# Lp pooling on one core: Square, reduce and Sqrt twice as wide, and the last store moved to the SP queue

## Chip, cores and metric

One core of one Trainium2 chip (trn2). Of its engines the kernel uses ACT (ScalarE), DVE (VectorE) and, to issue transfers, SP (SyncE); POOL is GpSimd. A transfer is issued on the queue of an engine (SP or ACT here) and carried out in packets by 16 DMA engines; it has landed when its last byte is in place. The metric is the device time of one execution in microseconds (us), median of the repeated runs. All runs quoted here are at granted clock 1.0. The profile's span is 1.7 to 2.3 us shorter than the time, in every run here (before: 393.7 and 395.92 for the profiled run), so spans and times are compared only with their own kind.

## The reference

```python
def setup_inputs():
    batch, channels, length = 32, 256, 4096
    return {"x": np.random.randn(batch, channels, length).astype(np.float32),
            "p": np.float32(2.0), "kernel_size": 4}

# for every window of four neighbours along the last axis
window = np.abs(x[:, :, start:end]) ** p
result[:, :, i] = (np.mean(window, axis=-1)) ** (1.0 / p)
```

134.22 MB come in, 33.55 MB go out, and there is almost nothing to compute: with p = 2, square, add four, take the root of a quarter.

## The kernel before

The input is a sequence of 32 tiles of 128 partitions by 8192 columns (4 MB each). Four input buffers; loads run on the SP queue, three or four ahead. Each tile is worked in two halves of 4096 columns: Square in place on ACT, add four neighbours on DVE, then one step later Sqrt on ACT. Outputs are collected in groups of four tiles (the last ones of 3 and 1) and stored once per group. I number tiles and loads from 0 to 31 and stores from 0 to 8.

```python
    W = 8192
    CH = 4096
    GROUP = 4
    LAST = 1
    # ... groups: seven of 4, one of 3, one of 1
    held = {len(groups) - 1 - LAST - j for j in range(2)}      # groups 6 and 7
    # ... in_pool 4 buffers, out_pool 2, last_pool 1
    def root(i, c):
        # ... o = this half's part of the group's output tile
        nc.scalar.activation(out=o, in_=o, func=Sqrt, scale=1.0 / k)
        if i == first + g - 1 and c + CH == W and group_of[i] not in held:
            nc.scalar.dma_start(out=out_block(group_of[i]), in_=ot)
    # ...
    for i in range(n):
        if i + 3 < n:
            load(i + 3)
        # ...
        for c in range(0, W, CH):
            xh = xts[i][:, c:c + CH]
            nc.scalar.activation(out=xh, in_=xh, func=Square)
            nc.vector.tensor_reduce(out=..., in_=xh.rearrange("p (n j) -> p n j", j=k), op=add)
            if pending is not None:
                root(*pending)
            pending = (i, c)
    root(*pending)
    for gi in sorted(held):
        nc.sync.dma_start(out=out_block(gi), in_=ots[gi])
```

Two stores (6 and 7) are held back and queued on SP behind the last load: they occupy the DMA engines while the last tile is computed. The very last store (8, 1 MB) goes out on the ACT queue.

Of the kernel before, what the change touches and what calls it, by code (L numbers as in the profile page):

```python
# [1 line left out]

# [4 lines left out]


@with_exitstack
def kernel(  # L10
    ctx: ExitStack,
    tc: tile.TileContext,
    x: bass.AP,
    p: float,
    kernel_size: int,
    out: bass.AP,
):








    nc = tc.nc

    assert float(p) == 2.0, "kernel specialized for p == 2"
    k = int(kernel_size)
    assert k == 4, "kernel specialized for kernel_size == 4"  # L30

    P = nc.NUM_PARTITIONS
    fp32 = mybir.dt.float32
    xf = x.rearrange("b c l -> (b c l)")
    of = out.rearrange("b c l -> (b c l)")
    total = xf.shape[0] // P

    W = 8192
    CH = 4096
    GROUP = 4  # L40
    LAST = 1
    n = total // W
    assert n * W == total


    groups = []
    i = 0
    while i < n - LAST:
        g = min(GROUP, n - LAST - i)
        groups.append((i, g))  # L50
        i += g
    groups += [(j, 1) for j in range(n - LAST, n)]
    held = {len(groups) - 1 - LAST - j for j in range(2)}
    group_of = {}
    for gi, (first, g) in enumerate(groups):
        for j in range(g):
            group_of[first + j] = gi

    in_pool = ctx.enter_context(tc.tile_pool(name="in_pool", bufs=4))
    out_pool = ctx.enter_context(tc.tile_pool(name="out_pool", bufs=2))  # L60
    last_pool = ctx.enter_context(tc.tile_pool(name="last_pool", bufs=1))
    ctx.enter_context(tc.manual_schedule())


    def x_block(i):
        first, g = groups[group_of[i]]
        block = xf[first * W * P:(first + g) * W * P].rearrange("(p w) -> p w", p=P)
        return block[:, (i - first) * W:(i - first + 1) * W]

    def out_block(gi):  # L70
        first, g = groups[gi]
        return of[first * W * P // k:(first + g) * W * P // k].rearrange("(p w) -> p w", p=P)

    xts = {}
    ots = {}

    def load(i):
        xt = in_pool.tile([P, W], fp32)
        nc.sync.dma_start(out=xt, in_=x_block(i))  # L79
        xts[i] = xt  # L80

    def root(i, c):
        first, g = groups[group_of[i]]
        ot = ots[group_of[i]]
        at = ((i - first) * W + c) // k
        o = ot[:, at:at + CH // k]
        nc.scalar.activation(  # L87
            out=o, in_=o, func=mybir.ActivationFunctionType.Sqrt, scale=1.0 / k,
        )
        if i == first + g - 1 and c + CH == W and group_of[i] not in held:  # L90
            nc.scalar.dma_start(out=out_block(group_of[i]), in_=ot)

    for i in range(3):
        load(i)

    pending = None
    for i in range(n):
        if i + 3 < n:
            load(i + 3)
        gi = group_of[i]  # L100
        first, g = groups[gi]
        if i == first:
            pool = last_pool if i >= n - LAST else out_pool
            ot = pool.tile([P, g * W // k], fp32)
            ots[gi] = ot
        for c in range(0, W, CH):
            xh = xts[i][:, c:c + CH]
            nc.scalar.activation(  # L108
                out=xh, in_=xh, func=mybir.ActivationFunctionType.Square,
            )  # L110
            at = ((i - first) * W + c) // k
            nc.vector.tensor_reduce(  # L112
                out=ots[gi][:, at:at + CH // k],
                in_=xh.rearrange("p (n j) -> p n j", j=k),
                axis=mybir.AxisListType.X, op=mybir.AluOpType.add,
            )
            if pending is not None:
                root(*pending)
            pending = (i, c)
    root(*pending)  # L120
    for gi in sorted(held):
        nc.sync.dma_start(out=out_block(gi), in_=ots[gi])


# [1 line left out]
_INS = ['x', 'p', 'kernel_size']  # L126
_OUTS = [((32, 256, 1024), 'float32')]

_NUMBERS = {'p': 2.0, 'kernel_size': 4}


# [26 lines left out]
```

## Time and profile before

| | before |
|---|---|
| time, median of 3 | 395.79 us |
| span | 393.7 us |
| ACT busy, DVE busy | 75%, 72% |
| DMA queues, share of 16 engines' span | 99.4% |

From the page of before: the span, the busy time of the engines, and the DMA queues (name, kind, packets, MB, and the time of their packets as a share of the span of 16 DMA engines; q1 is SP's queue, q10 is ACT's, q14 fetches instructions).

```profile
span 393.7 us, 357 instructions
DVE 282.8 (72%) x64; ACT 294.7 (75%) x130; POOL 0.2 (0%) x4
...
q1 hardware_dynamic: 4896, 141.56, 83.9%
q10 hardware_dynamic: 1008, 26.21, 15.5%
q14 instruction: 2, 0.02, 0.0%
```

No compute engine is near full, and 83.9% + 15.5% leaves the 16 DMA engines nothing. The packet records behind these lines (queue, start, duration and size of every packet) do not name the DMA engine. What is said below of single engines is inferred from which packet starts where another ends, and from the 16 small packets (4 bytes) that close every transfer, one for each engine; I call them completion packets. The records say how a packet's time is made: 309 ns for 8192 bytes, 912 for 24,576 and 1213 for 32,768, that is 301 ns per 8192 bytes and 8 or 9 ns fixed. At 1213 ns, 16 engines move 432 GB/s, so 167.77 MB take 388 us.

The groups of instructions on the same page (line, engine, operation, output from input, shapes, count | busy us, mean ns of one | idle time just before them, and what ended it), and three of the DMA issues (KB each, median us from issue to landing):

```profile
L112 DVE TENSOR_REDUCE ot<-xt 128x1024 f32<-128x4096 f32 x64 | 282.8, 4420 | 103.4 <-ACT xt L108 102.6
L108 ACT ACTIVATE xt<-xt 128x4096 f32<-128x4096 f32 x64 | 230.9, 3610 | 87.6 <-DMA xt<-in_x_dram 85.0
L87 ACT ACTIVATE ot<-ot 128x1024 f32<-128x1024 f32 x64 | 67.0, 1047 | 4.2 <-DVE ot L112 3.4
...
xt<-in_x_dram SPq DMA_DIRECT2D x32, 4096.0 KB, 35.9
...
out_dram<-ot SPq DMA_DIRECT2D x1, 3072.0 KB, 12.3
out_dram<-ot ACTq DMA_DIRECT2D x1, 1024.0 KB, 5.6
```

ACT waits 85.0 us in total before its Squares, and it waits for loads. The chain of waits of before (start us, us, what), one round from mid-span and its end:

```profile
152.67 35.95 DMA xt<-in_x_dram
188.64 3.62 ACT xt L108
192.26 0.95 ACT ot L87
193.21 3.51 ACT xt L108
196.74 4.43 DVE ot L112
201.19 35.94 DMA xt<-in_x_dram
...
386.17 1.06 ACT ot L87
```

This chain misleads if it is read as "12.5 us of compute in every 48". The load of 35.9 us stands in a queue of loads that land 9.7 us apart or more; compute frees a buffer long before its queue could run dry. Only the end is a real chain: the last load lands at 373.5, the last Sqrt ends at 387.2, the last store follows.

The last microseconds of before as stretches (stretch, its length, busy time of DVE, ACT and POOL with counts, clock, DMA share, GB/s; a packet counts in the stretch in which it starts, so a share can pass 1):

```profile
388.00:389.00 1.00, 0.00 (x0) 0.00 (x0) 0.00 (x0) 1.00 0.88 377
389.00:390.00 1.00, 0.00 (x0) 0.00 (x0) 0.00 (x0) 1.00 0.98 328
390.00:391.00 1.00, 0.00 (x0) 0.00 (x0) 0.00 (x0) 1.00 0.97 410
391.00:392.00 1.00, 0.00 (x0) 0.00 (x0) 0.00 (x0) 1.00 0.65 270
```

The DMA engines work on until the last store is out, although the compute is over at 387.2.

### The profile page before, as it was taken

How to read it: one execution, taken by the hardware profiler on the slowest of the kernel's cores; microseconds unless marked ns; L12 is line 12 of the kernel's file. 1: busy time of each engine (PE TensorE's matmuls, PEld its weight loads, DVE VectorE, ACT ScalarE, POOL GpSimd, SP SyncE). 2: the span in 40 equal slices, each digit the busy share in tenths (PEclk: the TensorE clock that was granted, in tenths of full speed). 3: DMA queues.
4: the chain of work that ended last, by engine and by line, in shares of the span. 5: the costliest groups of instructions: out<-in, count | busy, mean ns of one | idle time of the engine just before them, and what ended most of it. 6: DMA issues, size and time to landing. Idle time of an engine off the chain costs nothing.

```text
span 393.7 us, 357 instructions
## 1 busy us (share of the span) xinstructions
DVE 282.8 (72%) x64; ACT 294.7 (75%) x130; POOL 0.2 (0%) x4
## 2 busy tenths in 40 slices
DVE  0399996739976399764988559866598846999992
ACT  1699987469883798828988189863998819999981
POOL 0000000000000000000000000000000000000000
DMA  8999998999999999999999999999999999999997
GB/s 350 446 430 426 426 426 373 449 446 430 433 426 426 426 430 453 440 430 433 426 426 426 426 449 443 427 433 430 426 426 426 443 446 433 430 433 426 426 435 314
DMA packets 5906, 167.79 MB, mean 426 GB/s; under 512 B 656, under 2 KB 656, under 8 KB 656
## 3 DMA queue, kind: packets, MB, share of 16 engines
q1 hardware_dynamic: 4896, 141.56, 83.9%
q10 hardware_dynamic: 1008, 26.21, 15.5%
q14 instruction: 2, 0.02, 0.0%
HBM read 134.22 MB, written 33.55 MB: 426 GB/s over the span
## 4 chain that ended last, share of the span: by engine, by line
DMA 72%; ACT 17%; DVE 9%; SPq 0%; issue 0%; ACTq 0%
DMA xt<-in_x_dram 72%; ACT xt L108 14%; DVE ot L112 9%; ACT ot L87 2%; SPq L79 0%; ACTq L108 0%
## 5 line engine op out<-in xcount | busy, mean ns | idle before, releaser
L112 DVE TENSOR_REDUCE ot<-xt 128x1024 f32<-128x4096 f32 x64 | 282.8, 4420 | 103.4 <-ACT xt L108 102.6
L108 ACT ACTIVATE xt<-xt 128x4096 f32<-128x4096 f32 x64 | 230.9, 3610 | 87.6 <-DMA xt<-in_x_dram 85.0
L87 ACT ACTIVATE ot<-ot 128x1024 f32<-128x1024 f32 x64 | 67.0, 1047 | 4.2 <-DVE ot L112 3.4
L108 ACT ACT_TABLE_LOAD x1 | 1.3, 1283 | 0.7 <-PEq L139 0.7
L87 ACT ACT_TABLE_LOAD x1 | 1.3, 1283 | 0.0
L139 POOL MEMSET const-uint8-127<- 128x1 uint8 x1 | 0.1, 102 | 0.0
L139 POOL MEMSET const-bfloat16-1.0<- 128x1 bf16 x1 | 0.1, 101 | 0.0
L139 POOL MEMSET const-float32-0.0<- 128x1 f32 x1 | 0.1, 98 | 0.2 <-issue 0.2
L139 POOL MEMSET const-float32-1.0<- 128x1 f32 x1 | 0.1, 98 | 0.0
## 6 DMA issues: line engine op xcount, KB each, us to landing
xt<-in_x_dram SPq DMA_DIRECT2D x32, 4096.0 KB, 35.9
out_dram<-ot ACTq DMA_DIRECT2D x6, 4096.0 KB, 23.2
out_dram<-ot SPq DMA_DIRECT2D x1, 4096.0 KB, 34.1
out_dram<-ot SPq DMA_DIRECT2D x1, 3072.0 KB, 12.3
out_dram<-ot ACTq DMA_DIRECT2D x1, 1024.0 KB, 5.6
```

The lines of the kernel that those rows point to most:

```text
L87: nc.scalar.activation(out=o, in_=o, func=mybir.ActivationFunctionType.Sqrt, scale=1.0 / k,)
L108: nc.scalar.activation(out=xh, in_=xh, func=mybir.ActivationFunctionType.Square,)
L112: nc.vector.tensor_reduce(out=ots[gi][:, at:at + CH // k], in_=xh.rearrange("p (n j) -> p n j", j=k), axis=mybir.AxisListType.X, op=mybir. ...
L139: nc = _bacc.Bacc("TRN2", target_bir_lowering=False, num_devices=1)
```

## The change

Its intent: fewer, wider instructions where the time of one does not matter, narrow ones only where the end waits for them. Tiles 0 to 28 get one Square, one reduce and one Sqrt each (8192 columns); tiles 29 to 31 keep two halves. The loads themselves stay 8192 columns wide. The last store moves to the SP queue, and its output tile into a free input buffer.

```diff
-    W = 8192
-    CH = 4096
-    GROUP = 4
-    LAST = 1
+    W, O_W = 8192, 8192
+    X_SLOTS, O_SLOTS = 4, 2
+    slots = [[(W, [W])]] * 29 + [[(W, [4096, 4096])]] * 3
+    groups = [4] * 7 + [3, 1]
+    late = {6, 7, 8}
+    in_x = {8}
 # ... (tables of loads and groups, cut)
-        for c in range(0, W, CH):
-            xh = xts[i][:, c:c + CH]
-            nc.scalar.activation(
-                out=xh, in_=xh, func=mybir.ActivationFunctionType.Square,
-            )
+        for step in chunks:
+            v = xs[i][:, c:c + step]
+            nc.scalar.activation(out=v, in_=v, func=Act.Square)
 # ... (reduce and Sqrt alike, cut)
     root(*pending)
-    for gi in sorted(held):
-        nc.sync.dma_start(out=out_block(gi), in_=ots[gi])
+    for g in sorted(late):
+        store(g, nc.sync)
```

## The prediction

> **What bounds the kernel now.** The DMA engines, from end to end. The page gives ACT 75% and DVE 72% busy, but the DMA queues' share (part 3) is 83.9% + 15.5% = 99.4% of 16 engines' span. The trace's packet records agree: a 32,768-byte packet takes 1213 ns on its engine, so 16 engines move 432 GB/s, and 167.77 MB need 388 us of the 393.7 us span. The rest is 2.4 us until the first packet, about 1 us when the first store starts (at 58.8 us one packet of every engine takes 2.2 us), a few slow packets on single engines, and the last landing. The Trainium skill, "DMA: Bandwidth & Descriptors", section "Where 436 GB/s comes from", puts the ceiling at 435 GB/s; this trace agrees (432).
>
> The chain of waits reads "load 36 us, then Square, Sqrt, Square, reduce 12.5 us, then load". This is no compute bound: 36 us is three other loads (9.7 us each) in the same queue.
>
> **What the change does.** Loads stay 8192 columns wide (32 x 4 MB). Only Square, reduce and Sqrt become twice as wide for tiles 0 to 28; tiles 29 to 31 keep two halves. Each of the three goes from 64 to 35 instructions.
> - ACT: from Square (4096 columns, 3.61 us) and Sqrt (1024, 1.04 us) I estimate 0.84 ns a column and 0.18 us fixed, so wide ones 7.04 and 1.90 us. ACT saves about 29 x 0.36 = 10 us (294.7 to about 284). DVE: two of 4.42 become at most 8.84. Both have slack, so it is worth nothing.
> - Cost: Square and reduce of one tile no longer overlap, so a slot comes free 7.0 + 8.7 = about 15.8 us after landing, not 12.5. More than one whole load (about 13 us of data) is then still queued, before 17 us. The queue doesn't run dry. From issue to landing the load should fall from 35.9 to about 32.6 us, at the same rate.
> - Stores on ACT start about 4 us later; two output buffers absorb that.
> - The last load has the same two halves, so landing to last Sqrt stays at 13.6 us (373.6 to 387.2). Stores 6 and 7, queued behind the last load, keep the engines busy until about 389.5.
> - Last store (1 MB): before, it was issued on ACT at 387.26, and its packets start at 389.53, just as each engine ends with store 7. Now it follows store 7 on the SP queue: same engines, same bytes, issued perhaps 0.1 us later, and it may lose some packet jitter seen at 390.1 to 390.6. The Trainium skill, same page, "Issuing engines are not separate DMA queues", says only issue time is saved; the packet times fit that. Worth -0.4 to +0.3 us.
> - The last output tile sits in an input slot (that of load 28, long free) and waits for nothing.
>
> **On the critical path:** of the compute savings nothing; of the last store a few tenths.
>
> **Prediction: 395.7 us, range 395.1 to 396.4** (before 395.79). Faster by over 2%: 0.01; within 2%: 0.98; slower: 0.01.
>
> **What the profile should show if right:** DMA share still about 99% and 426 GB/s; ACT near 284 us; load issue to landing near 32.6 us; span 393.2 to 394.2; last load landing near 373.5; last Sqrt ending near 387.2; last store's packets beginning at 389.5 to 390 with no gap.
>
> **What would make it wrong:** a slot released so late that the queue runs dry (a stretch under 390 GB/s in mid-span); the last store waiting after store 7's last packet; a wide instruction far from twice the narrow one; or one engine of the 16 lagging by slow packets (0.2 to 1 us each), which is chance.

One correction to read it with: times of single packets in it ("58.8", "389.53", "2.4 us until the first packet", "390.1 to 390.6") were counted from a zero that I had set wrong; against the span's start they are 0.65 us earlier (58.2, 388.88, 1.75, 389.5 to 390.0). The same holds for the packet times in the expectations of the experiments. Durations and order are not touched. The 435 GB/s cited in it is that section's figure for the fabric; for transfers between HBM (the chip's main memory) and SBUF (the core's own), as here, the same section has a lower limit bind, about 358 GB/s. This kernel, alone on its core, moved 426 GB/s over the span: the measurement decides. From here on packet times are counted from the start of the first instruction, as on the page.

## The result, and the profile after

| | before | after |
|---|---|---|
| time, median (lowest to highest), 6 runs each | 395.73 (395.5 to 395.8) | 395.45 (394.88 to 395.88) |
| span of the profiled run | 393.7 | 393.4 |
| ACT busy, DVE busy, us | 294.7, 282.8 | 285.9, 278.3 |
| instructions in the profile | 357 | 240 |

The ratio is 0.9993 with a 95% interval of 0.998 to 1.0006. A ratio is the mean time of one kernel's runs over that of the other's of the same rounds, so not quite the ratio of the medians. No change is resolved.

The same parts of the page of after:

```profile
span 393.4 us, 240 instructions
DVE 278.3 (71%) x35; ACT 285.9 (73%) x72; POOL 0.2 (0%) x4
...
q1 hardware_dynamic: 5040, 142.61, 84.5%
q10 hardware_dynamic: 864, 25.17, 14.8%
q14 instruction: 1, 0.01, 0.0%
```

84.5% + 14.8% = 99.3%: the DMA engines are as full as before. The groups of instructions of after with shapes kept apart, and the DMA issues:

```profile
L109 DVE TENSOR_REDUCE ot<-xt 128x2048 f32<-128x8192 f32 x29 | 251.9, 8686 | 107.7 <-ACT xt L107 107.7
L107 ACT ACTIVATE xt<-xt 128x8192 f32<-128x8192 f32 x29 | 203.8, 7029 | 95.2 <-DMA xt<-in_x_dram 95.2
L83 ACT ACTIVATE ot<-ot 128x2048 f32<-128x2048 f32 x29 | 54.9, 1894 | 2.4 <-DVE ot L109 2.4
...
xt<-in_x_dram SPq DMA_DIRECT2D x32, 4096.0 KB, 32.7
...
out_dram<-ot SPq DMA_DIRECT2D x1, 3072.0 KB, 10.2
out_dram<-xt SPq DMA_DIRECT2D x1, 1024.0 KB, 3.8
```

ACT does 8.8 us less work and waits about that much longer for loads (95.2 + 0.9 us before all Squares instead of 87.6). The load's time from issue to landing fell from 35.9 to 32.7, which is no faster DMA: loads are issued some 3 us later, because Square and reduce of a tile no longer overlap.

The end of the chain of waits of after (pieces of under 0.1 us left out by the view):

```profile
343.88 7.04 ACT xt L107
350.94 8.70 DVE ot L109
359.66 1.91 ACT ot L83
361.57 3.52 ACT xt L107
365.11 4.43 DVE ot L109
...
387.66 1.06 ACT xt L83
```

Here is something I had not foreseen. From 343.9 us on, the chain holds no load at all. Tile 28 is wide: its reduce ends at 359.6, its Sqrt stands in ACT's queue ahead of tile 29's second half, and the narrow tiles behind do not make up for it before the end. The last Sqrt ends at 388.7, not 387.2. The last stretches of after show what it costs:

```profile
388.00:389.00 1.00, 0.00 (x0) 0.72 (x1) 0.00 (x0) 1.00 0.35 147
389.00:390.00 1.00, 0.00 (x0) 0.00 (x0) 0.00 (x0) 1.00 0.59 246
390.00:391.00 1.00, 0.00 (x0) 0.00 (x0) 0.00 (x0) 1.00 0.99 410
391.00:392.00 1.00, 0.00 (x0) 0.00 (x0) 0.00 (x0) 1.00 0.96 393
```

There is a dip at 388 to 390 (147 and 246 GB/s where before had 377 and 328). By the packet records, store 7 ends at 388.94 in the mean of the 16 engines and store 8 begins at 389.58; the low figure of 388 to 389 itself is mostly one of few starts, as packets that started in 387 still run. Yet after is not slower. Why, and whether wide instructions or the queue did anything at all, is what the experiments ask.

### The profile page after: what moved, and what is told of

Its sections match the earlier page's. It is cut to its first block, busy times and chain, and to the rows that moved or that the text cites. A ratio compares the mean times of both kernels' runs of the same rounds, so it can differ in the third digit from the quotient of the medians.

```text
span 393.4 us, 240 instructions
## 1 busy us (share of the span) xinstructions
DVE 278.3 (71%) x35; ACT 285.9 (73%) x72; POOL 0.2 (0%) x4
## 3 DMA queue, kind: packets, MB, share of 16 engines
q1 hardware_dynamic: 5040, 142.61, 84.5%
q10 hardware_dynamic: 864, 25.17, 14.8%
## 4 chain that ended last, share of the span: by engine, by line
DMA 59%; DVE 21%; ACT 18%; issue 0%; ACTq 0%
DMA xt<-in_x_dram 59%; DVE ot L109 20%; ACT xt L107 17%; DVE xt L109 1%; ACT ot L83 1%; ACT xt L83 0%; ACTq L107 0%
## 5 line engine op out<-in xcount | busy, mean ns | idle before, releaser
L109 DVE TENSOR_REDUCE ot<-xt 128x2048 f32<-128x8192 f32 (+1 forms) x33 | 269.5, 8168 | 109.1 <-ACT xt L107 109.1
L107 ACT ACTIVATE xt<-xt 128x8192 f32<-128x8192 f32 (+1 forms) x35 | 225.5, 6442 | 96.1 <-DMA xt<-in_x_dram 96.1
L83 ACT ACTIVATE ot<-ot 128x2048 f32<-128x2048 f32 (+1 forms) x33 | 59.1, 1791 | 2.5 <-DVE ot L109 2.4
L109 DVE TENSOR_REDUCE xt<-xt 128x1024 f32<-128x4096 f32 x2 | 8.8, 4420 | 0.2 <-ACT xt L107 0.2
L83 ACT ACTIVATE xt<-xt 128x1024 f32<-128x1024 f32 x2 | 2.1, 1048 | 3.5 <-DVE xt L109 3.5
## 6 DMA issues: line engine op xcount, KB each, us to landing
xt<-in_x_dram SPq DMA_DIRECT2D x32, 4096.0 KB, 32.7
```

The source lines that it names most:

```text
L83: nc.scalar.activation(out=o, in_=o, func=Act.Sqrt, scale=1.0 / k)
L107: nc.scalar.activation(out=v, in_=v, func=Act.Square)
L109: nc.vector.tensor_reduce(out=o, in_=v.rearrange("p (n j) -> p n j", j=k), axis=mybir.AxisListType.X, op=mybir.AluOpType.add,)
```

## The experiments

Twelve kernels, all correct, in three batches; each batch shared its chip and its runs of before (9 each). Medians of before in the batches: 395.49, 395.57 and 395.57. The last store's new place, in an input buffer, stays in all of them and is not tested alone. Where I say "slower, resolved", I mean that the 95% interval leaves 1. Except where said otherwise, an experiment is the changed kernel with one edit. My theory: the DMA engines bind, compute width is off the path, and only the tail and the engines' own disturbances can move the time. The rivals stand with each run.

This table is worked out from the packet records of each profiled run. "Fetches" are packets of queue 14 inside the span. "Last load" is when the completion packets of load 31 start, mean of 16 engines and the slowest. "Tail" is when the last store was issued, when its first packet started, and when the last packet of all ended. "Idle" is engine time without a packet from 376 us to that end, divided by 16.

| kernel | median us (runs) | ratio to before (95%) | fetches | last load mean, slowest | tail: issued, first packet, end | idle |
|---|---|---|---|---|---|---|
| before | see above | 1 | 2 | 372.16, 373.07 | 387.26, 388.86, 392.48 | 0.63 |
| after | 395.45 (6) | 0.9993 (0.998 to 1.0006) | 1 | 371.99, 372.54 | 388.74, 389.58, 392.24 | 0.72 |
| e1_narrow_sp | 395.68 (5) | 1.0003 (0.9989 to 1.0017) | 2 | 371.99, 372.92 | 387.11, 388.54, 392.33 | 0.87 |
| e2_wide_act | 395.19 (5) | 0.9997 (0.9984 to 1.0009) | 1 | 371.90, 373.04 | 389.24, 390.08, 392.75 | 1.32 |
| e3_wide_all | 397.32 (5) | 1.0047 (1.0034 to 1.0059) | 1 | 371.93, 372.42 | 390.68, 391.51, 394.18 | 2.64 |
| e4_eighths | 396.79 (5) | 1.0032 (1.0019 to 1.0044) | 6 | 371.91, 373.85 | 389.27, 390.10, 393.27 | 1.82 |
| e10_pool_fetch | 400.18 (4) | 1.0118 (1.0104 to 1.0131) | 9 | 372.03, 377.26 | 393.48, 394.32, 396.98 | 5.35 |
| e12_long_tail | 395.16 (5) | 0.9989 (0.9976 to 1.0001) | 1 | 371.79, 372.38 | 386.55, 388.44, 391.79 | 0.52 |

The mean landing of the last load is the column to look at first: 371.8 to 372.2 in all of them, whatever the width and whatever the busy time of ACT.

### The two parts of the change alone: e1_narrow_sp and e2_wide_act

Only the queue (narrow instructions everywhere):

```diff
-    slots = [[(W, [W])]] * 29 + [[(W, [4096, 4096])]] * 3
+    slots = [[(W, [4096, 4096])]] * 32
```

> After with 4096-column instructions everywhere, last store still on the SP queue: the queue move alone. My theory (the DMA queues bound it, compute width is off the path, only the tail counts): ACT busy back to about 295 us, last Sqrt ends near 387.3 us instead of 388.7, the last store's packets start about 389.5 to 390 without the 0.3 us of idle engines that after shows; time 395.0 to 395.6 us, at or just under after. Rival (the wide instructions gave the 0.3 us): time goes back to before, 395.7 to 395.8. Both differences are near the scatter of runs (0.3 to 1 us), so the place of the last packets decides, not the time.

Only the width (the last store on ACT):

```diff
-    late = {6, 7, 8}
+    late = {6, 7}
```

> After with the last store back on the ACT queue: the width alone. My theory: last Sqrt ends near 388.7 as in after, issue about 388.75, first packets of the last store about 2.2 us later, near 390.9, end of packets 393.1 to 393.6; time 395.4 to 396.1, that is 0 to 0.6 us over after. Rival (SP and ACT queue alike for the last store): within 0.1 us of after, packets start as in after, near 390.3.

Measured: 395.68 and 395.19, against 395.49 of before; neither ratio leaves 1. As expected for e1, ACT busy is back at 294.7, the last Sqrt ends at 387.1, and there is no gap: the last store's packets start at 388.54 (0.3 us sooner than expected, by the corrected zero), while other engines are at store 7 until 389.87. The time is 0.08 us above my range and does not tell the two theories apart, as the expectation said it might not.

For e2 I was wrong and its rival right about the queue. I had expected the first packet of the last store about 2.2 us after its issue on ACT. It came after 0.84 us (389.24 to 390.08), exactly as on SP in after (388.74 to 389.58, 0.84). (The last Sqrt too came 0.5 us later than expected, at 389.2: load 28, with which this chain begins, closed at 343.90 on its slowest engine, 343.40 in after.) The longer delay in before (1.60) was not the queue's: its 16 engines were still busy with store 7. What follows: the last store has to be issued 0.84 us before the engines run empty, on either queue. In after they run empty near 388.9 (store 7's completion packets, mean 388.94), so an issue after about 388.1 (the difference) should cost time, and 388.74 is 0.6 us too late. The equal delays agree with the Trainium skill, "DMA: Bandwidth & Descriptors", section "Issuing engines are not separate DMA queues", by which transfers run on the same 16 DMA engines whichever engine starts them.

### No narrow tail: e3_wide_all

```diff
-    slots = [[(W, [W])]] * 29 + [[(W, [4096, 4096])]] * 3
+    slots = [[(W, [W])]] * 32
```

> 8192-column instructions in the last three tiles too. My theory: last load still lands near 373.2; then Square 7.0, reduce 8.7, Sqrt 1.9 in series: last Sqrt ends near 390.9, last store issued about 391, its packets start about 393, span near 396.2, time about 398.2 us (397.6 to 398.8), 2.2 to 3.3 over after. DMA engines idle some 2 to 4 us at the end. Rival (width matters nowhere, the stores behind the last load cover the tail): 395.5.

Measured 397.32, ratio 1.0047 (1.0034 to 1.0059): slower, resolved. The end of its timeline (start us, us, engine, line, operation):

```profile
380.02 8.69 DVE L109 TENSOR_REDUCE xt<-xt 128x2048 f32<-128x8192 f32 x1 [1.03 <-ACT xt L107]
...
388.74 1.91 ACT L83 ACTIVATE xt<-xt 128x2048 f32<-128x2048 f32 x1 [6.95 <-DVE xt L109]
390.68 0.33 SPq L80 DMA_DIRECT2D out_dram<-xt  x1
```

The order is as expected, the last store issued at 390.7 instead of 391. The time is below my range (397.6 to 398.8) by 0.3 us: I had again put in about 2 us from issue to first packet, where 0.83 were measured. So width does matter where the end waits for it; the rival, that the queued stores cover any tail, falls.

### More instructions in the middle: e4_eighths

```diff
-    slots = [[(W, [W])]] * 29 + [[(W, [4096, 4096])]] * 3
+    slots = [[(W, [1024] * 8)]] * 29 + [[(W, [4096, 4096])]] * 3
```

> Instructions of 1024 columns (eight a tile) in the first 29 tiles, tail as in after. ACT busy should rise from 286 to about 360 us (Square 1.04, Sqrt 0.40 us each, 0.19 us fixed each, 232 of each), DVE to about 305. My theory: time unchanged, 395.0 to 396.2, DMA share 99%. Rival (the fixed cost of instructions is on the path): time rises with ACT, by 10 us or more.

Measured 396.79 (396.46 to 396.95), above my range of 395.0 to 396.2. ACT busy rose to 334.3 us (85%; neighbouring instructions overlap, so not 360), DVE to 309.4. The rival's 10 us did not come, but something cost 1.3 us. The packet records show it: the mean landing of the last load is unchanged (371.91), but two of the 16 engines land it 1.6 to 1.9 us behind the other fourteen. And queue 14, which carries instructions, has six packets of 8192 bytes in the span instead of one; each takes 309 ns or a little more, and the next packet on that engine takes 1.57 to 1.88 us instead of 1.21. The slowest engine is done with store 7 at 390.81, and its eight packets of store 8 then set the end, 393.27. A new theory, then: fetching instructions uses the same DMA engines, and a kernel that fills them waits for the slowest. Its rival: ACT and DVE were busier. The next experiment separates them.

### Instructions that nothing waits for: e10_pool_fetch

```diff
+    spare = warm_pool.tile([P, 16], fp32, name="spare")
+    for _ in range(1000):
+        nc.gpsimd.memset(spare, 0.0)
```

> After with 1000 small memsets on POOL, which nothing waits for: instructions alone, without ACT or DVE work. Theory F (instruction fetches ride on the DMA engines: each 8192-byte packet of queue 14 holds up its engine by about 0.6 us, as in the run with eighths, where two engines were 1.6 to 1.9 us behind the other fourteen at the last load): 6 to 9 packets on queue 14 in the span, one or two engines behind the others by 1 to 5 us at the last load's landing, mean landing unchanged (372.6), time 396 to 399. Rival (the eighths were slower because ACT and DVE were busier): no engine falls behind, last load lands at 373.2, time as after, 395.2 to 395.5.

Measured 400.18 (400.09 to 400.64), ratio 1.0118: 4.7 us slower than after (4.6 than before of its own batch) for memsets that run on an idle engine and are all over at 170 us. From its page:

```profile
span 398.2 us, 1241 instructions
DVE 278.3 (70%) x35; ACT 285.9 (72%) x72; POOL 112.4 (28%) x1004
...
q14 instruction: 9, 0.07, 0.0%
```

ACT and DVE are as busy as in after to the tenth. Queue 14 has nine packets instead of one, eight of them while POOL works, one for about every 127 memsets (892 of them start between the first and the eighth). At the last load the slowest engine lands at 377.26, the second slowest at 372.13 and the mean at 372.03. One engine fell behind a little with each fetch, 5.13 us in the end, or 0.64 us for each of eight; it lags 0.9 us at 41 us and 5.2 at 193, and no more after that. The stretches of e10 near the end, when fifteen engines have finished store 6 and wait (share 0.08):

```profile
382.00:384.00 2.00, 1.97 (x2) 1.97 (x2) 0.00 (x0) 1.00 0.08 33
384.00:386.00 2.00, 2.00 (x1) 2.00 (x2) 0.00 (x0) 1.00 0.51 217
```

The engines starve there because tile 31 can't be computed before the lagging engine's part of it is in, and stores 7 and 8 wait for the compute. So theory F holds, its expected size (1 to 5 us of lag, 396 to 399) a little short; the rival falls, since it had to leave the time at 395.2 to 395.5. The Trainium skill, "Runtime: NRT & Kernel Launch", section "Instruction fetch mechanics", says that a sequencer drives its own DMA queue for instructions in 16 KiB blocks and that crossing a block is mostly hidden. A queue for instructions alone (14) is in this trace; that each sequencer has its own is not shown. The packets seen are of 8192 bytes and come one at a time, and the cost is not hidden here, where the DMA engines are the bottleneck; the measurement decides.

This also names what I had called chance in before and after: one fetch at 250.8 us moves before's slowest engine from 0.42 to 0.98 us behind the median engine, and one at 260.3 us moves after's from 0.31 to 0.6. Before's other fetch (159.8 us) fell on an engine that was not the slowest. Not all lag is of this kind: e2 lands its last load with the slowest engine 1.26 us behind the median engine, and 0.57 of it were there before its one fetch, at 260.8 us.

### Where the stall at the first store comes from: e6, e7, e8, e11

In all kernels one or two packets of every engine are slow some 1.7 to 3.6 us before the first large store's own packets begin (at 58 us in before, most of them 2.1 to 2.4 us instead of 1.2; at 62 in after, mostly 1.9 to 2.3). It costs an engine about 1 us (1.1 in before, 1.0 in after, 0.7 in e8); without it a kernel could beat both. Is it the first use of the ACT queue, the first write, or what?

```diff
# e6_early_act_load: a tiny load on the ACT queue first
+    nc.scalar.dma_start(out=warm, in_=xf[0:P * 16].rearrange("(p w) -> p w", p=P))
# e7_all_sp: every store on SP
-            store(g, nc.scalar)
+            store(g, nc.sync)
# e8_first_sp: only the first store on SP
+            store(g, nc.sync if g == 0 else nc.scalar)
# e11_early_write: 8 KB of zeros stored first, overwritten later
+    nc.vector.memset(spare, 0.0)
+    nc.scalar.dma_start(out=of[0:P * 16].rearrange("(p w) -> p w", p=P), in_=spare)
```

> After with one tiny load (8 KB) on the ACT queue before everything. Asks what stalls all 16 engines for about 1 us when the first store goes out (packets of 2.0 to 2.3 us instead of 1.2 at 60 us). Theory A, first use of the ACT queue: the stall at 60 us is gone, a stall in the first microseconds takes its place or none; last load lands up to 1 us earlier, 372.2 instead of 373.2; time 394.4 to 395.5. Theory B, first write to HBM: the stall stays at 60 us; last load at 373.2, time as after.

> After with every store on the SP queue, none on ACT. Theory A (first use of ACT queue): no packet over 2 us anywhere after the start, last load lands near 372, time 394.4 to 395.2. Theory B (first write): stall at the first store stays, time 395.0 to 395.7. Loads wait behind the stores' semaphores on SP, but a load is issued 10 us apart, so no run dry in either.

> After with only the first store on the SP queue, the other five on ACT. Theory A (first use of the ACT queue): the stall moves from 60 us to the second store, about 112 us. Theory B (first write): it stays with the first store, which now starts its packets later, behind the loads queued, about 85 to 95 us. Time as after within 0.4 us in both.

> After with an 8 KB store of zeros to the output at the very start (overwritten later by the first real store, which waits for it). The runs before showed that the stall of about 1 us of all engines goes with the first store, on whichever queue. Theory B1 (it belongs to the first write to HBM, of any size and place): the stall moves to the first microseconds, none at 60 us; last load lands near 372.2 to 372.7; time 394.5 to 395.2. Rival B2 (it belongs to the first large store, its size or its being in the way of loads): the stall stays near 60 us, time as after, 395.2 to 395.5.

| | median us | ratio to before (95%) | slow packets of all engines at |
|---|---|---|---|
| e6_early_act_load | 395.44 | 0.9996 (0.9983 to 1.0008) | 63 us |
| e7_all_sp | 395.56 | 0.9998 (0.9985 to 1.0012) | 78 us |
| e8_first_sp | 395.22 | 0.999 (0.9977 to 1.0002) | 77 us |
| e11_early_write | 395.51 | 0.9998 (0.9986 to 1.0011) | 62 to 63 us |

Theory A (first use of the ACT queue) falls three times: an early load on that queue leaves the stall where it was, a kernel that never uses the queue still has it, and moving only the first store moves the stall with it (77 us: that store stands behind queued loads; I had expected 85 to 95). Only a shadow is left at the second store of e8 (four packets of 1.4 us at 113 to 123 us). Theory B1 (any first write) falls with e11: 8 KB written at the start, and the stall stays. What remains is "the first large store"; whether its size, its addresses or its meeting with the loads counts is open. e7 also shows that the choice of queue for all six early stores moves the time by nothing that these runs resolve.

### A better tail: e12_long_tail, and everything together: e13_early_tail_group

```diff
-    slots = [[(W, [W])]] * 29 + [[(W, [4096, 4096])]] * 3
+    slots = [[(W, [W])]] * 27 + [[(W, [4096, 4096])]] * 5
```

> After with two halves in the last five loads instead of three. Theory (in after the wide reduce of load 28 holds up the Squares of the last three loads, so the last Sqrt ends 1.5 us late and the engines stand idle 0.6 us before the last store): last Sqrt near 387.2, idle before the last store under 0.15 us, last packets end 0.3 to 0.6 us earlier than in after (392.9), at the pace of the slowest engine; time 394.9 to 395.2. Rival (the tail of after costs nothing): as after, 395.4.

Measured 395.16 (395.05 to 395.30), ratio 0.9989 (0.9976 to 1.0001). Here the backlog is gone: tile 29's first Square waits for its load again. The last Sqrt starts at 385.47 and the last store goes out at 386.55, early enough. That Square and the end of its timeline, and its last stretches:

```profile
353.50 3.62 ACT L107 ACTIVATE xt<-xt 128x4096 f32<-128x4096 f32 x1 [0.41 <-DMA xt<-in_x_dram]
...
386.55 0.33 SPq L80 DMA_DIRECT2D out_dram<-xt  x1
```

```profile
388.00:389.00 1.00, 0.00 (x0) 0.00 (x0) 0.00 (x0) 1.00 0.55 229
389.00:390.00 1.00, 0.00 (x0) 0.00 (x0) 0.00 (x0) 1.00 0.97 410
...
391.00:392.00 1.00, 0.00 (x0) 0.00 (x0) 0.00 (x0) 1.00 0.12 49
```

The dip of after at 388 to 390 is gone in the packet records: in e12 the last store's packets start at 388.44, while store 7's slowest engine is still at work until 389.34. (The low figure of 388 to 389 is of few starts, not of empty engines: a packet of 912 ns that started in 387 fills most of it.) The last packet of all ends at 391.79, 0.45 us before after's. All five runs of e12 are below all nine of before in its batch (395.43 to 396.0), but the interval just includes 1. It is the best version found; its lead of about 0.4 us over before is not resolved by the ratio.

e13 adds the early write and one Sqrt per group of four for groups 0 to 5.

> Early write and long tail together, and one Sqrt per group of four loads for the first six groups (18 fewer ACT instructions). Theory: gains add, 1 us of the stall and 0.5 of the tail, and with fewer instructions no or one packet of instruction fetch in the span: last packets end near 391.3, time 393.8 to 394.6, under both kernels. Rival: stall or fetch stays, time 394.8 or more.

Measured 395.26 (395.13 to 395.46), ratio 0.9992 (0.998 to 1.0005): its rival was right. The early write does not take the stall away, as e11 shows, and the 18 instructions fewer only put the one fetch off, from 263 to 315 us.

### The size of the load: e5_half_loads

```diff
-    slots = [[(W, [W])]] * 29 + [[(W, [4096, 4096])]] * 3
-    groups = [4] * 7 + [3, 1]
+    slots = [[(4096, [4096]), (4096, [4096])]] * 32
+    groups = [8] * 7 + [6, 2]
```

> After with the loads themselves halved: 64 loads of 4096 columns, so packets of 16,384 bytes. From the packet times in the traces (8192 B 309 ns, 24,576 B 912, 32,768 B 1213: 301 ns per 8192 B and 8 or 9 ns fixed) I expect 611 ns a packet and 256 more packets an engine: 2.3 us more, 0.3 more for the 32 further completion packets; mean landing of the last load 372.6 + 2.6 = 375.2, time 397.5 to 398.3. Rival (packet size has no part, DMA rate fixed by bytes): time as after.

Measured 397.78 (397.48 to 397.9), ratio 1.0056 (1.0042 to 1.0069). Packets of 16,384 bytes take 612 ns (expected 611), and the mean landing of the last load moves from 371.99 to 374.13 us. The expectation of 2.6 us later was 0.5 too much, the time is in its range. This is the control: half as many *instructions* in the middle move nothing that can be resolved; *loads* of half the size cost 2.3 us against after (2.2 against before of the batch), which fits the 8 to 10 ns that each of 256 more packets an engine adds.

## Why the prediction was right

**The bound (right).** Widths of 1024, 4096 and 8192 columns (e4, before and e1, after and e3) leave the mean landing of the last load at 371.9 to 372.2, with ACT busy from 285 to 334 us. Work taken off ACT in this kernel is worth nothing, as its idle time before Squares, put down to loads, said. The Trainium skill, "Perfetto Trace Analysis", section "Optimizing Scalar/DVE Operations", says that larger operations can improve throughput "if the engine is saturated"; here it is not, and nothing improves.

**Sizes of the instructions (right).** Predicted 7.04, 1.90 and 8.7 us; measured 7.03, 1.89 and 8.69. ACT fell to 285.9 instead of "about 284". Load to landing 32.7, predicted 32.6.

**The last Sqrt at 387.2 (wrong, and cancelled).** The step that failed is "The last load has the same two halves, so landing to last Sqrt stays at 13.6 us". It looked only at tile 31. The wide tile 28 keeps DVE until 359.6, and three narrow tiles are too few to catch up: the last Sqrt ended at 388.7, about 15.6 us after the landing (0.5 us earlier a landing, 1.5 later an end than in before). A narrow tile takes ACT 9.05 us there (second Squares at 361.48, 370.53, 379.58), and loads land 9.7 us apart, so a tile makes up for only 0.65 us. e12 shows it, since with two more narrow tiles the last Sqrt ends at 386.5. How many it takes depends on where the last wide tile falls: in e12 the next load came later (Squares at 321.89 and 334.00), and the backlog was gone after two narrow tiles; four were not run. The loss is small because the engines had store 7 to do until about 388.9: 0.6 us of empty engines.

**"Last store's packets beginning at 389.5 to 390 with no gap" (wrong).** Read 388.9 to 389.4 after the correction of the zero. They began at 389.58, and there was a gap. Under "what would make it wrong" the last store waiting after store 7's last packet was listed; it happened, at a size inside the range.

**Why it cancels.** In before the last store ends on 15 engines between 391.61 and 391.94, and one straggler sets the end, at 392.48: it is done with store 7 at 390.02 and has eight packets of 309 ns to go. In after all engines wait for the late store, start it together, and end within 0.14 us, at 392.24. The gap ate the straggler's lag: idle time in the tail is 0.63 us an engine in before and 0.72 in after. The jitter that the prediction hoped to lose is lost (14 of the last store's 128 packets took 0.41 to 0.75 us in before, none in e1 and after), but it was not on the straggler, so its loss does not move the end. The prediction had neither the gap nor the straggler in its sum. That the time lies so near its middle is in part luck: a lag that it had called chance covers its error of 1.5 us in the last Sqrt. These single profiles account for 0.2 to 0.3 us between the two profiled runs; they do not prove that after is faster, which the runs leave open.

**"One engine of the 16 lagging by slow packets ..., which is chance" (wrong in its cause).** A part of the lag has a cause, instruction fetches, and e10 shows that it can be made 5 us large.

## What to carry to other kernels

In this kernel, whose DMA queues' shares sum to 99%, the width of the compute left the mean landing where it was. In one like it, look at the mean landing of the last load, then only at the tail. In the tail, give the last output to its queue before the stores ahead of it run out (here 0.84 us before), and begin the narrow instructions enough tiles ahead that the last wide one's backlog is gone (five were enough here, three were not). On DMA engines as full as these, instructions are traffic too: a thousand memsets on an idle engine cost 4.7 us.

## What the Trainium skill lacked or had wrong

- "Runtime: NRT & Kernel Launch", section "Instruction fetch mechanics": it gives 16 KiB blocks and a cost mostly hidden. The trace shows packets of 8192 bytes, one for about 127 POOL instructions, each costing its DMA engine 0.64 us; eight of them on one engine made a DMA-bound kernel 4.7 us slower.
- No page that I found has the stall with the first large store: one or two packets of all 16 engines take up to 2.7 us instead of 1.21 (e12), 0.7 to 1.1 us an engine with loads of this size, not moved by the first use of the ACT queue or by an early 8 KB write. Its cause is open.
- "DMA: Bandwidth & Descriptors", section "Why small descriptors are slow (HBM only)", names a fixed overhead for each packet but weighs it for small ones alone (27% at 256 bytes). For packets of 8 to 32 KB the traces have 8 to 10 ns each, and 256 more packets an engine cost 2.1 us of landing time and 2.3 us of time (e5).
